# Start addresses of the matmuls' moving operands in a four-layer hybrid trunk

## The chip, the cores and the metric

The kernel runs on one core of a Trainium2 chip. The metric is the device time of one execution, in microseconds (us). Each number given for a kernel as a whole is the median of its runs; the profile is one further execution, with its own time beside it.

## The reference

Four residual layers work on 256 tokens of width 1024 in float32. Layers 0 and 3 mix tokens by an RWKV-7 recurrence, layer 1 by stick-breaking attention, layer 2 by attention over 64 keys picked per query. Each is followed by a SwiGLU feed-forward block (FFN) of inner width 2816.

```python
def swiglu(h, w_gu, w_down):
    g, u = jnp.split(h @ w_gu, 2, axis=-1)
    return (jax.nn.silu(g) * u) @ w_down
...
    for i in range(DEPTH):
        kind, j = i % N_MIXERS, i // N_MIXERS
        h = rms_norm(x, norm_mix[i])
...
        x = x + y
        x = x + swiglu(rms_norm(x, norm_ffn[i]), ffn_w_gu[i], ffn_w_down[i])
```

Most of the arithmetic is matrix products of the 256 tokens with weights that are read from memory once: 401 weight pieces of 512 KB each.

## The kernel before, in words

**Pieces.** `piece` (line 906) brings 128 rows by 1024 columns of weights into a tile of the group `raw`, rounds them to the type fp32r into a tile `wh` (the high part), and puts what the rounding lost into a tile `wl` (the low part). The activations are split in the same way. A product is then built from fp32r matmuls: high by high, high by low, low by high. There are four slots each of `raw`, `wh` and `wl`. A slot of `wh` or `wl` is 1056 columns wide; the piece begins at column 16 of a `wh` slot and at column 4 of a `wl` slot, that is 64 and 16 bytes behind the slot's start, whatever reads it.

**Stationary and moving.** A matmul has a stationary operand, which a weight load puts into the array first, and a moving operand, which is then streamed from SBUF. In the profile's names, `gate<-xg,wh` writes the PSUM tile `gate`, and the two names behind the arrow are its operands, in order of the moving one and the stationary one.

- In `gemm1` and the FFN (lines 948 and 1068) the pieces are stationary and the activations move: `xg` (normed activations, high and low halves side by side), or `h` (the FFN's inner activations, also high and low side by side). One matmul of 512 columns reads high and low together against `wh`, and one of 256 columns reads the high half against `wl`. These two make a pair with the same moving start. The names are `gate`, `up`, `dn` (the down product) and `qk`.
- In `gemm2` and `out_half` the pieces are stationary too, but high and low halves of the activations lie apart, so that three matmuls of 256 columns make a unit: `kp`, `rp`, `po`.
- In `v_gemm` (line 1629) and `by_tokens` (line 1745) it is the other way round: `xg` is stationary and the pieces move, 512 columns at a time: `vps`, `k`, `q`, `qi`.

**The FFN.** For each of 11 blocks of 256 inner columns, `gate` and `up` take 8 pairs per 128 columns, so that a phase has 352 pairs; `h` is spread over three tiles: groups `SA` (blocks 0 to 3), `SZ` (4 to 7) and `PR` (8 to 10). The down product then runs over the 22 halves of `h` for each of 8 output tiles: 172 pairs, and for the last 4 halves of the last tile three matmuls of 256 columns each. Up to two output tiles are worked on in turn.

**Order and addresses.** A planner (`Plan`) records all operations and sets their order on every engine from its own cost table, dependences and a table of nudges. Its costs look at shapes, types and engines, not at addresses. `Plan.emit` then asks a pool for the SBUF tiles, in the order of the names in `LAYOUT` (line 65), and the pool gives each the next free address, in steps of 32 bytes. In the weight products above, each moving read lies a multiple of 1024 bytes behind the start of its tile or piece, so where such a matmul starts to read, modulo 512, is set by where the tile or piece starts.

Of the kernel before, what the change touches and what calls it, by code (L numbers as in the profile page):

```python
# [14 lines left out]
F32R = mybir.dt.float32r  # L15
# [18 lines left out]
PIECE = 1024  # L34
# [22 lines left out]
for _n, _w in CONSTS:  # L57
# [5 lines left out]


LAYOUT = (
    "ones xt0 chmask xt1 xt2 xt3 sqa_0 QC_0 sq_0 s0_0 raw_0 s1_0 t_0 s6_0 raw_1 raw_2 t_1 t_2 t_3 raw_3 wh_0 wl_0 "
    "wh_1 wh_2 wh_3 t2_0 xm_0 t2_1 xm_1 PR_0 xm_2 consts0 wl_1 xm_3 identb t2_2 wl_2 t_4 t2_3 wl_3 s7_0 xb_0 SZ_0 "
    "t2_4 dc_0 vf0 vf1 vf3 vf2 t_5 t_6 t_7 kc0_0 kc1_0 kc2_0 SA_0 eps_rms lim eps_gn vecs omka kks_0").split()


class Region:
# [249 lines left out]
class Plan:  # L321
# [15 lines left out]
    def unit(self, at_once=1, ns=0.0):  # L337

        plan = self

        class Unit:
            def __enter__(self):
                plan.unit_op = Op("tensor")
                plan.unit_op.ns = ns

            def __exit__(self, *_):
                op, plan.unit_op = plan.unit_op, None
                op.cost /= at_once
                op.cost = op.ns or op.cost
                plan._add(op)  # L350

        return Unit()
# [478 lines left out]
def trunk(ctx: ExitStack, tc: tile.TileContext, xT_in, vecs_in, wts, lora_in, consts_in, id32_in, nqk_in, outT, order, layers=None):  # L831
# [11 lines left out]
    def T(shape, group=None, name="t", dtype=F32):  # L843
        return plan.tile(sb, [P] + list(shape), dtype, group, name)
# [7 lines left out]
    def bank(name, group="ps"):  # L852
        return plan.tile(psum, [P, 512], F32, group, name, "psum")
# [8 lines left out]
    ones = T([P], name="ones")  # L862
# [23 lines left out]
    identb = T([P], name="identb", dtype=BF16)  # L886
    eps_rms, eps_gn = T([1], name="eps_rms"), T([1], name="eps_gn")
    anye.memset(eps_rms, 1e-6)
    lim = T([2], name="lim")
# [3 lines left out]
    omka = T([2, NC], name="omka")  # L893
    for j in range(2):
        dve.tensor_scalar(omka[:, j, :], vt[:, VIDX[f"ka{j}"], :], -1.0, 1.0, op0=ALU.mult, op1=ALU.add)
    chmask = T([2 * NCH, C], name="chmask")
# [4 lines left out]
    def f(ap):  # L901
        return ap.bitcast(F32)


    def piece(key):

        i = len(order)
        order.append(key)
        r = T([PIECE], "raw", f"raw{i}")
        sp.dma_start(r, wts[i])  # L910
        h, l = (T([PIECE + 32], g, f"{g}{i}", F32R)[:, at:at + PIECE] for g, at in (("wh", 16), ("wl", 4)))
        anye.copy(h, r)
        dve.tensor_tensor(l, r, f(h), op=ALU.subtract)
        return h, l
# [26 lines left out]
    def v3(t, n):  # L941
        return t.rearrange("p (k m) -> p k m", k=n)
# [12 lines left out]
    def gemm1(key, x, name, group="g"):  # L955


        out = bank(name, group)
        wh, wl = [v3(t, NC) for t in piece(key)]
        for c in range(NC):  # L960
            with unit():
                pe.matmul(out, wh[:, c], flat(x[:, c]), start=(c == 0), stop=False)
                pe.matmul(out[:, :S], wl[:, c], x[:, c, 0], start=False, stop=(c == NC - 1))
        return out

    def gemm2(key, xs, name):

        out = bank(name, "g")
        for c in range(NC):
            if c % 4 == 0:  # L970
                wh, wl = [v3(t, 4) for t in piece(key + (c // 4,))]
            with unit():
                for i in range(2):
                    sl = slice(i * P, (i + 1) * P)
                    mm3(out[:, i * S:(i + 1) * S], (wh[:, c % 4, sl], wl[:, c % 4, sl]), xs(c),
                        start=(c == 0 and i == 0), stop=(c == NC - 1 and i == 1))
        return out

    def out_half(key, half, xs, after):

        for j in range(4):
            o = bank("po", "g")
            wh, wl = [v3(t, 4) for t in piece(key + (half, j))]
            for k in range(4):
                with unit():
                    for n in range(2):
                        sl = slice(n * P, (n + 1) * P)
                        mm3(o[:, n * S:(n + 1) * S], (wh[:, k, sl], wl[:, k, sl]), xs(k),
                            start=(k == 0 and n == 0), stop=(k == 3 and n == 1))
            dve.tensor_tensor(xt[j], xt[j], ab(o), op=ALU.add)  # L990
            if half == 1:
                after(j)
# [636 lines left out]
    def v_gemm(vt_, key, xs, rsc, k):  # L1629

        o = [bank("vps", "g") for tb in range(2)]
        for c in range(NC):
            if c % 2 == 0:
                wh, wl = [v3(t, 2) for t in piece(key + (c // 2,))]
            xh, xl = xs(c)
            with unit():
                for tb in range(2):
                    tsl = slice(tb * P, (tb + 1) * P)
                    pe.matmul(o[tb], xh[:, tsl], wh[:, c % 2, :], start=(c == 0), stop=False)
                    pe.matmul(o[tb], xh[:, tsl], wl[:, c % 2, :], start=False, stop=False)  # L1640
                    pe.matmul(o[tb], xl[:, tsl], wh[:, c % 2, :], start=False, stop=(c == NC - 1))
        for tb in range(2):
            anye.scale(vt_[:, k, tb, :], o[tb], rsc[:, tb:tb + 1])
# [10 lines left out]
    def stick(layer, after):  # L1654
# [13 lines left out]
        for p in range(8):  # L1668
# [9 lines left out]
            for n in {0: [0], 4: [1]}.get(p, ()):  # L1678
                v_gemm(vt_, ("sv", n), xs, rsc, n)
# [32 lines left out]
    def dsa(layer, after):  # L1712
# [21 lines left out]
        for i in range(2):  # L1734
            ct_, st_ = tables(1024 + 256 * i), tables(1152 + 256 * i)
            g = nqk[:, i:i + 1]
# [9 lines left out]
        def by_tokens(n, name):  # L1746

            o = [bank(name, "g") for tb in range(2)]
            for c in range(0, NC, 2):
                wh, wl = [v3(t, 2) for t in piece(("dt", n, c // 2))]  # L1750
                for tb in range(2):
                    tsl = slice(tb * P, (tb + 1) * P)
                    for i in range(2):
                        xh, xl = xs(c + i)
                        with unit():
                            pe.matmul(o[tb], xh[:, tsl], wh[:, i, :], start=(c + i == 0), stop=False)
                            pe.matmul(o[tb], xh[:, tsl], wl[:, i, :], start=False, stop=False)
                            pe.matmul(o[tb], xl[:, tsl], wh[:, i, :], start=False, stop=(c + i == NC - 1))
            return o
# [17 lines left out]
        def queries_keys(kind, half):  # L1777

            o = by_tokens(2 * kind + half, "kq"[1 - kind])
            at = qt_[:, 2 * kind + half]  # L1780
            r = rr[:, 2 * kind + half]
            for tb in range(2):
                anye.scale(at[:, tb], o[tb], rsc[:, tb:tb + 1])
            for tb in range(2):
                sq = t2("sq")
                act.activation(flat(sq), at[:, tb], AF.Square)
                dve.tensor_reduce(r[:, tb], heads(flat(sq)), axis=AX.X, op=ALU.add)
            act.activation(r, r, AF.Ln, bias=eps_rms, scale=1.0 / HD)
            act.activation(r, r, AF.Exp, scale=-0.5)
            if kind == 0:  # L1790
                for i in range(2):
                    anye.scale(rq[:, half, i], r, (1 - 2 * i) * HD ** -0.5)
            for tb in range(2):
                if kind:
                    dve.tensor_tensor(heads(at[:, tb]), heads(at[:, tb]), r[:, tb][:, :, None].to_broadcast([P, 8, HD]), op=ALU.mult)
                turned(at[:, tb], kind, tb, qk_[:, 4 * half:4 * half + 4, kind, tb * P:(tb + 1) * P])


        ips = by_tokens(6, "qi")
        rs, rsc = rstd_bcast(), rstd_col()  # L1800
        wh, wl = [v3(t, 8) for t in piece(("dk",))]
# [57 lines left out]
        for p in range(8):  # L1859
# [4 lines left out]
            if p % 4 == 0:  # L1864
                values = by_tokens(4 + p // 4, "vps")
                for tb in range(2):
                    anye.scale(vt_[:, p // 4, tb], values[tb], rsc[:, tb:tb + 1])
# [10 lines left out]
            for hh in range(2):  # L1878
# [14 lines left out]
                t = bank("pT")  # L1893
# [207 lines left out]
```

## Time and profile before

| what | value |
|---|---|
| median of 3 runs | 1349.35 us (1347.35 to 1350.13) |
| the profiled execution | 1346.9 us, with a span of 1345.0 us |
| granted TensorE clock | 1.000 of full speed over the whole span |
| weight pieces | 401 of 512 KB, 3.9 us median from issue to landing |
| FFN phases | gate and up 182.7 to 303.7 us, dn 303.7 to 365.2 us in layer 0; much the same three times more |

The matmul engine is PE, its weight loads are PEld, the vector engine is DVE, the scalar engine is ACT. A row of the groups names the tiles, the shape of the array used, the columns and the count, then the busy time and the mean duration of one. A matmul's duration runs from its start to a modelled end, so it holds a tail that the next matmul overlaps. The chain of waits, which lists stretches of PE with their length and the number of matmuls, gives the time that each truly takes up.

### The profile page before, as it was taken

To read this page: it belongs to the slowest core of one execution; us is meant where nothing else is said; L and a number is where in the kernel's file an instruction comes from. 1 tells how busy PE (TensorE), PEld (TensorE's weight loads), DVE (VectorE), ACT (ScalarE), POOL (GpSimd) and SP (SyncE) were. 2 spreads that over 40 slices of the span, in tenths; PEclk is the share of its full clock that TensorE was granted. 3 is DMA by queue.
4 is the path that set the end of the run, shared out by engine and by line. 5 is a ranking of instruction groups with operands and counts; after the bars stand their busy time and mean duration, and the time that the engine had idled before them with its cause. 6 is when DMAs were issued, how large, how long until landed. Compare 5 with 4: busy or idle time off the path is not lost.

```text
span 1345.0 us, 26070 instructions
## 1 busy us (share of the span) xinstructions
PE 1324.5 (98%) x10480; PEld 1159.3 (86%) x10480; DVE 1116.6 (83%) x1932; ACT 776.6 (58%) x1301; POOL 9.1 (1%) x22
## 2 busy tenths in 40 slices
PE   9999899999999999999999999999999999999998
PEld 7997798888888898888888788888899877988887
DVE  8998789886676779996679988887589997998864
ACT  7955665555466755444456876555378366655542
POOL 0000000000000000000000000000000000000000
PEclk9999999999999999999999999999999999999999
DMA  6423255665654446565654535666544232556653
GB/s 243 145 81 125 75 174 188 193 198 176 208 171 157 123 152 192 190 192 201 197 185 138 178 129 186 191 193 197 189 128 133 73 112 76 176 188 190 193 189 120
DMA packets 61336, 220.09 MB, mean 164 GB/s; under 512 B 6816, under 2 KB 8352, under 8 KB 60960
## 3 DMA queue, kind: packets, MB, share of 16 engines
q1 hardware_dynamic: 61216, 218.44, 50.6%
q8 instruction: 82, 1.34, 0.4%
q14 instruction: 38, 0.31, 0.1%
HBM read 217.36 MB, written 1.05 MB: 162 GB/s over the span
## 4 chain that ended last, share of the span: by engine, by line
PE 83%; DVE 12%; ACT 3%; issue 1%; DMA 1%; SPq 0%; DVEq 0%; ACTq 0%
PE dn L827 18%; PE gate L827 18%; PE up L827 18%; PE po L827 6%; PE qk L827 3%; PE vps L827 3%; PE kp L827 3%; PE z L827 2%; DVE inv L827 2%; PE q L827 2%; PE k L827 2%; DVE xtmp L827 1%; DVE SB L827 1%; PE rp L827 1%; DVE wl L827 1%
## 5 line engine op out<-in xcount | busy, mean ns | idle before, releaser
L827 ACT CAST wh<-raw 128x1024 fp32r<-128x1024 f32 x351 | 365.9, 1049 | 332.4 <-PE dn L827 93.7
L827 DVE TENSOR_TENSOR wl<-raw,wh 128x1024 fp32r<-128x1024 f32 x383 | 461.1, 1220 | 83.5 <-ACT wh L827 67.1
L827 PE MATMUL gate<-xg,wh 128*128 128x512 f32 x704 | 260.5, 390 | 0.0
L827 PE MATMUL up<-xg,wh 128*128 128x512 f32 x704 | 260.2, 390 | 0.0
L827 PE MATMUL dn<-h,wh 128*128 128x512 f32 (+1 forms) x720 | 244.4, 388 | 0.0
L827 PE MATMUL dn<-h,wl 128*128 128x256 f32 x704 | 196.1, 278 | 0.0
L827 PE MATMUL up<-xg,wl 128*128 128x256 f32 x704 | 194.5, 276 | 0.0
L827 PE MATMUL gate<-xg,wl 128*128 128x256 f32 x704 | 194.5, 276 | 0.0
L827 PEld LDWEIGHTS dn<-h,wh 128*128 128x128 f32 x720 | 134.2, 188 | 29.3
L827 PEld LDWEIGHTS up<-xg,wh 128*128 128x128 f32 x704 | 132.2, 188 | 27.6
L827 PEld LDWEIGHTS gate<-xg,wh 128*128 128x128 f32 x704 | 132.2, 188 | 27.4
L827 PEld LDWEIGHTS dn<-h,wl 128*128 128x128 f32 x704 | 132.3, 188 | 0.0
L827 PEld LDWEIGHTS up<-xg,wl 128*128 128x128 f32 x704 | 132.2, 188 | 0.1
L827 PEld LDWEIGHTS gate<-xg,wl 128*128 128x128 f32 x704 | 132.1, 188 | 0.1
L827 PE MATMUL vp<-xv,raw 128*128 128x256 f32 x256 | 57.4, 382 | 0.6 <-PE qct L827 0.6
L827 ACT CAST h<-gus 128x512 fp32r<-128x512 f32 x42 | 26.1, 621 | 55.3 <-DVE gus L827 55.0
L827 DVE TENSOR_TENSOR gus<-gus,rstd 128x512 f32<-128x512 f32 x88 | 57.0, 683 | 0.1
L827 PEld LDWEIGHTS vp<-xv,raw 128*128 128x128 f32 x256 | 47.8, 190 | 8.1 <-PE qct L827 0.8
L827 DVE TENSOR_TENSOR h<-gus,h 128x512 fp32r<-128x512 f32 x44 | 30.4, 691 | 25.5 <-ACT h L827 25.5
L827 PE MATMUL rp<-prx,wh 128*128 128x256 f32 x256 | 50.3, 296 | 0.0
L827 PE MATMUL kp<-kx,wh 128*128 128x256 f32 x256 | 47.4, 285 | 0.9 <-DVE kx L827 0.8
L827 PE MATMUL po<-yhl,wh 128*128 128x256 f32 x256 | 47.8, 288 | 0.0
(327 smaller groups left out, 2350.6 us busy)
## 6 DMA issues: line engine op xcount, KB each, us to landing
raw<-in_wts_dram SPq DMA_DIRECT2D x401, 512.0 KB, 3.9
lora<-in_lora_dram SPq DMA_DIRECT2D x2, 1280.0 KB, 10.5
xt<-in_xT_dram SPq DMA_DIRECT2D x4, 256.0 KB, 3.7
lora<-in_lora_dram SPq DMA_DIRECT2D x2, 512.0 KB, 6.5
inv<-in_id_dram SPq DMA_DIRECT2D x2, 512.0 KB, 3.5
out_dram<-xt SPq DMA_DIRECT2D x8, 128.0 KB, 1.9
sbt<-in_consts_dram SPq DMA_DIRECT2D x1, 512.0 KB, 3.7
consts<-in_consts_dram SPq DMA_DIRECT2D x1, 288.0 KB, 9.6
```

Of the source, the lines that this page charges most:

```text
L827: getattr(getattr(nc, o.eng), method)(*map(real, args), **{k: real(a) for k, a in kw.items()})
```

## The change

All instructions, their order on every engine and all their waits stay as they are; row by row, the five engines' lists are the same once the numbers in tile names are left out. Two kinds of address change.

```diff
 LAYOUT = (
-    "ones xt0 chmask xt1 xt2 xt3 sqa_0 QC_0 sq_0 s0_0 raw_0 s1_0 t_0 s6_0 raw_1 raw_2 t_1 t_2 t_3 raw_3 wh_0 wl_0 "
-    "wh_1 wh_2 wh_3 t2_0 xm_0 t2_1 xm_1 PR_0 xm_2 consts0 wl_1 xm_3 identb t2_2 wl_2 t_4 t2_3 wl_3 s7_0 xb_0 SZ_0 "
-    "t2_4 dc_0 vf0 vf1 vf3 vf2 t_5 t_6 t_7 kc0_0 kc1_0 kc2_0 SA_0 eps_rms lim eps_gn vecs omka kks_0").split()
+    "identb dc_0 ones xt0 chmask xt1 xt2 xt3 sqa_0 QC_0 sq_0 s0_0 s1_0 raw_0 raw_1 raw_2 raw_3 xb_0 SZ_0 PR_0 SA_0 "
+    "eps_rms lim eps_gn t_0 s6_0 t_1 t_2 t_3 wh_0 wl_0 wh_1 wh_2 wh_3 t2_0 xm_0 t2_1 xm_1 xm_2 consts0 wl_1 xm_3 t2_2 "
+    "wl_2 t_4 t2_3 wl_3 s7_0 t2_4 vf0 vf1 vf3 vf2 t_5 t_6 t_7 kc0_0 kc1_0 kc2_0 vecs omka kks_0").split()
...
-    def piece(key):
+    def piece(key, home=(16, 4)):
...
-        h, l = (T([PIECE + 32], g, f"{g}{i}", F32R)[:, at:at + PIECE] for g, at in (("wh", 16), ("wl", 4)))
+        h, l = (T([PIECE + 32], g, f"{g}{i}", F32R)[:, at:at + PIECE] for g, at in zip(("wh", "wl"), home))
...
-                wh, wl = [v3(t, 2) for t in piece(key + (c // 2,))]
+                wh, wl = [v3(t, 2) for t in piece(key + (c // 2,), (0, 0))]
...
-                wh, wl = [v3(t, 2) for t in piece(("dt", n, c // 2))]
+                wh, wl = [v3(t, 2) for t in piece(("dt", n, c // 2), (0, 0))]
```

With the tiles in the new order, these are the byte addresses in a partition that the built programs give, and what is left of them modulo 512:

| slot | moving operand it holds | before | mod 512 | after | mod 512 |
|---|---|---|---|---|---|
| `xb` | `xg` (gate, up, qk) | 163584 | 256 | 77312 | 0 |
| `SA` | `h` blocks 0 to 3 | 211072 | 128 | 126464 | 0 |
| `SZ` | `h` blocks 4 to 7; `prx` (rp) | 179968 | 256 | 93696 | 0 |
| `PR` | `h` blocks 8 to 10; `kx` (kp) | 116608 | 384 | 110080 | 0 |
| `s0`, `s1` | `yhl`, `ohl` (po), `xv` (vp) | 44160, 56448 | 128 | 44544, 52736 | 0 |
| `xt0` to `xt3`, `sqa`, `sq`, `QC` | float32 operands | 5248 and on | 128 | 5632 and on | 0 |
| `raw` 0 to 3 | none (`vp` loads it as weights) | 52352, 73984, 78080, 85248 | 128, 256, 256, 256 | 60928 and on | 0 |
| `wh` 0 to 3, slot start | pieces in vps, k, q, qi | 89344, 97792, 102016, 106240 | 256, 0, 128, 256 | 155392, 163840, 168064, 172288 | 256, 0, 128, 256 |
| `wl` 0 to 3, slot start | pieces in vps, k, q, qi | 93568, 136320, 143872, 151168 | 384, 128, 0, 128 | 159616, 185984, 193280, 200576 | 384, 128, 256, 384 |

Pieces that are read as moving operand start at the slot's start after the change, and 64 (`wh`) or 16 bytes (`wl`) behind it before. Pieces that are stationary keep their 64 and 16 bytes. The small tiles `t`, `t2` and `xm`, which are moving operands of some float32 matmuls, and `s6` (128 modulo 512 before and after) are not put on multiples of 512.

## The prediction, as it was put on record

> **What bounds the kernel now.** I read the page first: who is busy, and what the chain that ended last is made of.
>
> ```profile
> span 1345.0 us, 26070 instructions
> PE 1324.5 (98%) x10480; PEld 1159.3 (86%) x10480; DVE 1116.6 (83%) x1932; ACT 776.6 (58%) x1301; POOL 9.1 (1%) x22
> ...
> PE 83%; DVE 12%; ACT 3%; issue 1%; DMA 1%; SPq 0%; DVEq 0%; ACTq 0%
> PE dn L827 18%; PE gate L827 18%; PE up L827 18%; PE po L827 6%; PE qk L827 3%; PE vps L827 3%; PE kp L827 3%; PE z L827 2%; DVE inv L827 2%; PE q L827 2%; PE k L827 2%; DVE xtmp L827 1%; DVE SB L827 1%; PE rp L827 1%; DVE wl L827 1%
> ```
>
> PE is busy for 98% of the span and makes up 83% of the chain; gate, up and dn alone are 54%. No instruction moves, so only what each matmul takes can change the time, and a nanosecond on one of these is a nanosecond of the kernel, if the engines that prepare the pieces keep up. The stretches of layer 0 say how much room they have (busy us of PE, PEld, DVE, ACT, POOL; then clock, DMA share, GB/s):
>
> ```profile
> 182.70:303.70 121.00, 121.00 (x714) 107.06 (x713) 108.66 (x169) 63.93 (x84) 0.00 (x0) 1.00 0.59 191
> 303.70:365.20 61.50, 61.50 (x359) 54.00 (x358) 39.66 (x54) 29.86 (x36) 0.00 (x0) 1.00 0.58 190
> ```
>
> In gate and up DVE is busy 108.66 of 121.0 us, so PE could gain some 12 us there (10%) before DVE set the pace; in dn there is far more room.
>
> Next the groups by shape, for the products that the new addresses touch. A matmul's duration has a tail that the next one overlaps, and the tail is the same for equal work, so a difference of means is a difference of pace.
>
> ```profile
> L827 PE MATMUL gate<-xg,wh 128*128 128x512 f32 x704 | 260.5, 390 | 0.0
> L827 PE MATMUL dn<-h,wh 128*128 128x512 f32 x688 | 238.9, 393 | 0.0
> L827 PE MATMUL dn<-h,wl 128*128 128x256 f32 x704 | 196.1, 278 | 0.0
> L827 PE MATMUL gate<-xg,wl 128*128 128x256 f32 x704 | 194.5, 276 | 0.0
> L827 PE MATMUL rp<-prx,wl 128*128 128x256 f32 x128 | 35.9, 281 | 0.0
> L827 PE MATMUL po<-yhl,wl 128*128 128x256 f32 x128 | 35.9, 280 | 0.0
> L827 PE MATMUL kp<-kx,wl 128*128 128x256 f32 x128 | 36.0, 281 | 0.0
> ```
>
> The same work takes longer in dn than in gate: 3 ns more per 512 columns, 2 ns more per 256. Gate reads one tile that starts at 256 modulo 512; dn reads three that start at 128, 256 and 384. The chain of waits, in order of time, gives the true pace (start, us, matmuls):
>
> ```profile
> 281.81 2.38 PE gate L827 x14
> 304.62 60.88 PE dn L827 x354
> 602.11 60.52 PE dn L827 x353
> 921.49 60.56 PE dn L827 x354
> 1280.53 60.60 PE dn L827 x354
> ```
>
> A gate pair takes 2.38 / 7 = 0.340 us.
>
> **Where dn loses it.** Three short windows of one dn phase (groups by shape in the window) tell more than its mean. From the planner's order: at 336.2 to 339.2 us two output tiles take turns and all moving starts are at 128 modulo 512; at 339.30 the first reads from `SZ` (256) come in and alternate with those at 128; at 318.3 to 323.6 the starts are 384 and 128, then 128 alone.
>
> ```profile
> L827 PE MATMUL dn<-h,wh 128*128 128x512 f32 x10 | 3.4, 389 | 0.0
> L827 PE MATMUL dn<-h,wl 128*128 128x256 f32 x10 | 2.8, 276 | 0.0
> ...
> L827 PE MATMUL dn<-h,wh 128*128 128x512 f32 x8 | 2.8, 395 | 0.0
> L827 PE MATMUL dn<-h,wl 128*128 128x256 f32 x7 | 2.0, 280 | 0.0
> ...
> L827 PE MATMUL dn<-h,wh 128*128 128x512 f32 x16 | 5.7, 396 | 0.0
> L827 PE MATMUL dn<-h,wl 128*128 128x256 f32 x16 | 4.5, 279 | 0.0
> ```
>
> In the first window dn has gate's pace, though two outputs take turns, so turns are not what costs. From the moment on when starts differ by 128 modulo 256, a pair costs 6 + 4 = 10 ns more. The third window is a warning: starts that agree modulo 256, and still the slow pace (7 + 3). So the slow pace is something that PE falls into when the residue changes and that can outlast the change. With every `h` tile at 0 the trigger inside dn is gone; whether PE is ever in the slow pace on entering dn is left.
>
> **The change part by part.**
>
> *dn.* A chain stretch of 354 matmuls is 171 pairs and four units of three. At gate's pace that is 171 x 0.340 = 58.1 us, and 4 x 0.355 = 1.4 us for the units (3 x 0.113 by gate's pace for 256 columns, plus 4 to 5 ns each as the wl rows of rp, po and kp show): 59.6. The four phases took 60.88, 60.52, 60.56 and 60.60, so the excess is 1.3 + 1.0 + 1.0 + 1.0 = 4.3 us. That is the most that this term can give if 0 acts like 128, 256 and 384 do; the least is 0, if the slow pace stays as in the third window. Gate, which has only one residue, loses next to nothing, so I take three quarters: -3.3 us.
>
> *Pieces as moving operand.* Rows of the moving side (min/median/max):
>
> ```profile
> L827 PE MATMUL gate<-xg,wh x704: 388/389/587, 182.7 to 1280.0; 128*128 128x512 f32 x176
> L827 PE MATMUL vps<-wh,xg x128: 387/397/581, 372.5 to 764.0; 128*128 128x512 f32 x128
> L827 PE MATMUL vps<-wl,xg x64: 388/393/398, 372.9 to 763.8; 128*128 128x512 f32 x64
> L827 PE MATMUL k<-wh,xg x64: 387/396/400, 676.2 to 730.2; 128*128 128x512 f32 x64
> L827 PE MATMUL q<-wh,xg x64: 387/397/584, 689.7 to 743.4; 128*128 128x512 f32 x64
> L827 PE MATMUL qi<-wh,xg x32: 388/394/482, 662.6 to 675.2; 128*128 128x512 f32 x32
> L827 PE MATMUL k<-wl,xg x32: 388/389/398, 676.4 to 730.0; 128*128 128x512 f32 x32
> ```
>
> `wh` at 64 bytes off takes 5 to 8 ns over gate's median, `wl` 16 bytes off 0 to 4. Brought to 389 all would give 8 x 128 + 7 x 64 + 8 x 64 + 5 x 32 + 4 x 64 = 2400 ns. But the slots themselves are not moved to 512: `wh` then starts at 256, 0, 128, 256 and `wl` at 384, 128, 256, 384, so high and low of a unit often differ by 128 modulo 256, which is what cost dn 6 ns (395 against 389). Between -2.4 us and, should all 288 `wh` reads pay a few ns more, +1 us, I take -0.7 us: most of the two effects cancel.
>
> *gate, up, qk.* One moving tile before and after; 256 becomes 0. If 0 is no better or worse than the three other residues: 0. Bounds are with the rivals.
>
> *kp, rp, po.* Their starts agree already (384, 256, 128 in each), and all have 280 or 281: the residue makes no difference among them. 0.
>
> *The rest.* Engines that write or read the moved tiles:
>
> ```profile
> L827 DVE TENSOR_TENSOR wl<-raw,wh x383: 1199/1218/1258, 13.1 to 1333.4; 128x1024 fp32r<-128x1024 f32 x192
> L827 ACT CAST wh<-raw x351: 1031/1049/1093, 11.0 to 1332.3; 128x1024 fp32r<-128x1024 f32 x176
> L827 PE MATMUL vp<-xv,raw x256: 379/379/483, 85.4 to 1092.4; 128*128 128x256 f32 x128
> ```
>
> These run over `raw` at 128 and 256 and over all slots of `wh` and `wl` with hardly any spread, and a float32 matmul has one duration; 0 for all three, hidden or not. `raw` lands at other addresses; ACT waits for few landings, so a small change there is covered.
>
> The sum: -3.3 - 0.7 = -4.0 us. On the profiled execution, 1346.9 - 4.0 = 1342.9; it lies 2.45 us under the median, so the median goes to 1349.35 - 4.0 = 1345.4 us. Nothing is late next: DVE has its room, and the order is the planner's as before.
>
> **The rivals.**
>
> *A start at 512 is a case of its own* (18%). The fp32r matmul of 256 columns never takes less than 276, while the warm-up's bf16 one of equal shape gets to 272:
>
> ```profile
> L1935 PE MATMUL warm_o<-warm_x x66: 272/283/421, 1.2 to 1132.7; 128*128 128x256 bf16 x66
> ```
>
> So the fp32r stream pays at least 4 ns per 256 columns, at every start that the trace has. No start at 0 is among them. If those 4 ns were the two 512-byte boundaries that 1024 bytes cross from a start off 512, a start on it crosses one fewer, 2 ns less for each of some 6,500 fp32r matmuls: -13 us, with dn's -4 about 1332 us. If all of it went (4 ns per 256 columns, 8 per 512), 2,600 x 8 + 3,800 x 4 = 36 us, and DVE's room in gate and up would still cover it: 1313. Against it: 128, 256 and 384 pay alike, and so do pieces 16 and 64 bytes off (minimum 387 or 388), though they lie across more boundaries of any smaller size.
>
> *Nothing changes* (20%). The slow pace of dn may come from the sequence of products or last by itself, as at 318.3 us; then about 1349 us. [...]
>
> *Gate and up fall into the slow pace* (12%), slower. They keep 0.340 only as long as PE stays in step. If 0 against stationary pieces at 64 and 16 bytes off, which the trace does not have for these slots, were out of step, 1,408 pairs x 10 ns = 14 us: 1363; with half of the pairs 1356. It is slower from 30% of the pairs on, where it eats dn's gain. Against it: 128, 256 and 384 all reach 389 and 276 with the same pieces; for it, the third window shows that the slow pace holds without a change of residue.
>
> **How the numbers follow.** My own case (50%) spans 1344 to 1349, as its terms go from -5.4 to 0; about 1345.4 is the likeliest. About 0.2%, 2.7 us, is what a measurement can tell from no change. My case passes it three times in four, the case of its own always: 0.37 + 0.18 = 0.55 faster. The same: a quarter of mine, all of "nothing", a little of the slow pace: 0.34. Slower: 0.11. For 8 in 10 the range takes my case, nothing, the half-size slow pace, and the 512 case to its 13 us: 1330 to 1355.
>
> **What would show it.** Right: the dn rows come to 389 to 391 and 276, its four chain stretches to 59.6 to 60 us, gate stays at 390 and 276, rp, po and kp at 280 to 281. The 512 case: gate falls under 388 and 275. Slow pace: gate at 395 and 280. "Nothing": dn stays at 393 and 278. The forecast is wrong if gate's rows move at all, or if dn's do not.

## The result, and the profile after

| what | before | after |
|---|---|---|
| median, first comparison | 1349.74 us (1347.35 to 1350.29, 4 runs) | 1342.28 us (1341.22 to 1343.40, 4 runs) |
| ratio, 95% interval | | 0.9950 [0.9934, 0.9966] |
| median, second comparison | 1347.06 us (23 runs) | 1342.65 us (5 runs) |
| ratio, 95% interval | | 0.9964 [0.9951, 0.9977] |
| profiled execution, span | 1346.9 us, 1345.0 us | 1343.4 us, 1341.5 us |

The changed kernel is faster. The two medians differ by 7.5 and by 4.4 us; what both intervals allow is 0.9951 to 0.9966, or 4.6 to 6.6 us. Most of what sets the two differences apart is the kernel before, whose median is 1349.74 us over 4 runs and 1347.06 us over 23. The page first:

```profile
span 1341.5 us, 26070 instructions
PE 1319.9 (98%) x10480; PEld 1157.1 (86%) x10480; DVE 1117.1 (83%) x1932; ACT 776.3 (58%) x1301; POOL 9.3 (1%) x22
...
PE gate L827 18%; PE up L827 18%; PE dn L827 17%; PE po L827 7%; PE vps L827 3%; PE qk L827 3%; PE kp L827 3%; PE z L827 2%; DVE inv L827 2%; PE k L827 2%; PE q L827 2%; DVE xtmp L827 1%; DVE SB L827 1%; PE rp L827 1%; PE chain L827 1%
```

PE lost 4.6 us of busy time, and DVE and ACT nothing (1117.1 for 1116.6 and 776.3 for 776.6); dn went from 18% of the chain to 17%. The groups by shape of the kernel after (busy us, mean ns of one):

```profile
L827 PE MATMUL gate<-xg,wh 128*128 128x512 f32 x704 | 260.3, 390 | 0.0
L827 PE MATMUL dn<-h,wh 128*128 128x512 f32 x688 | 234.4, 389 | 0.0
L827 PE MATMUL dn<-h,wl 128*128 128x256 f32 x704 | 194.4, 276 | 0.0
L827 PE MATMUL gate<-xg,wl 128*128 128x256 f32 x704 | 194.4, 276 | 0.0
L827 PE MATMUL rp<-prx,wl 128*128 128x256 f32 x128 | 35.9, 281 | 0.0
L827 PE MATMUL po<-yhl,wl 128*128 128x256 f32 x128 | 35.9, 280 | 0.0
```

The two rows of dn went from 393 and 278 to 389 and 276, which is gate's pace; the other rows shown here stand where they stood. The chain of waits of the kernel after, in order of time (start, us, matmuls):

```profile
307.21 59.55 PE dn L827 x354
...
920.38 59.59 PE dn L827 x354
...
1278.06 59.56 PE dn L827 x354
```

These three stretches were 60.88, 60.56 and 60.60: 1.33, 0.97 and 1.04 us less. The other phase is cut by a wait in this execution (50.22 us, 295 matmuls, in its longest part); in the profile of the second comparison it is whole:

```profile
600.35 59.56 PE dn L827 x354
```

It was 60.52 us for one matmul fewer, so dn gave 1.33 + 0.96 + 0.97 + 1.04 = 4.3 us. The moving rows of the kernel after (min/median/max):

```profile
L827 PE MATMUL gate<-xg,wh x704: 389/389/584, 185.4 to 1277.6; 128*128 128x512 f32 x176
L827 PE MATMUL vps<-wh,xg x128: 388/392/583, 373.8 to 763.6; 128*128 128x512 f32 x128
L827 PE MATMUL vps<-wl,xg x64: 387/395/398, 374.2 to 763.4; 128*128 128x512 f32 x64
L827 PE MATMUL k<-wh,xg x64: 387/392/404, 676.0 to 729.7; 128*128 128x512 f32 x64
L827 PE MATMUL q<-wh,xg x64: 387/392/581, 689.5 to 742.9; 128*128 128x512 f32 x64
L827 PE MATMUL k<-wl,xg x32: 387/393/398, 676.2 to 729.5; 128*128 128x512 f32 x32
```

High pieces as moving operand came down from 396 or 397 to 392, low ones went up from 389 to 393 (k) and from 393 to 395 (vps). To add up such small pieces I took, for every matmul in the trace, the time from its start to the start of the next, less gate's pace (226.7 ns for 512 columns, 113.3 for 256, that is 340 ns for a pair), and left out matmuls that come out more than 25 ns over it, as waits. What a duration holds beyond that time, its tail, has a median of 161 to 163 ns in every one of these products, before and after. Summed by product, in us:

| | before | after |
|---|---|---|
| dn | 4.66 | 0.23 |
| vps, k, q, qi (pieces move) | 2.11 | 1.53 |
| gate, up, qk | 1.08 | 0.64 |
| kp, rp, po | 6.77 | 6.75 |

That is 5.5 us off the matmuls' pace, but the two profiled executions differ by only 1346.9 - 1343.4 = 3.5 us. Part of the rest is in the first stretch. The windows, before and then after (busy us of PE, PEld, DVE, ACT, POOL; granted clock, DMA share, GB/s):

```profile
10.00:20.00 10.00, 8.84 (x46) 7.57 (x45) 10.00 (x19) 9.10 (x16) 1.34 (x1) 1.00 0.81 333
```

```profile
10.00:20.00 10.00, 7.97 (x31) 6.17 (x29) 9.41 (x21) 8.97 (x16) 1.52 (x1) 0.83 0.85 338
```

In these 10 us the kernel after got 31 matmuls done where the one before did 46; its gate starts at 185.4 us, not at 182.7. The 0.83 is a mean: the granted clock was 0.50 for 3.4 us, and full before and after.

```profile
13.30:16.70 3.40, 3.40 (x8) 2.73 (x9) 3.40 (x7) 3.39 (x4) 0.08 (x1) 0.50 1.04 413
```

The clock is not the whole delay. The first product of the layer, `lora_in`, started at 11.69 us, where it had started at 10.43, so the kernel was 1.3 us late before the clock fell; over the spell at half clock `lora_in` fell back from 1.27 to 2.95 us behind the kernel before, 1.7 us more, and the waits between there and gate made 2.7 us of the 3.0. The profile of the second comparison, of the very same kernel, has 1.00 there, starts gate at 182.6, and has a span of 1340.6 us, 4.4 under before's:

```profile
L827 PE MATMUL gate<-xg,wh x704: 389/389/584, 182.6 to 1276.6; 128*128 128x512 f32 x176
```

So this late start is the execution's and not the change's. Of the 5.5 us that the starts give, 4.4 us show in that span; where the other 1 us goes, among the waits, was not followed.

### The profile page after: what moved, and what is told of

Same layout as the page of the kernel before. It is cut to its first block, busy times and chain, and to the rows that moved or that the text cites. A ratio compares the mean times of both kernels' runs of the same rounds, so it can differ in the third digit from the quotient of the medians.

```text
span 1341.5 us, 26070 instructions
## 1 busy us (share of the span) xinstructions
PE 1319.9 (98%) x10480; PEld 1157.1 (86%) x10480; DVE 1117.1 (83%) x1932; ACT 776.3 (58%) x1301; POOL 9.3 (1%) x22
## 4 chain that ended last, share of the span: by engine, by line
PE 84%; DVE 11%; ACT 2%; issue 1%; DMA 1%; SPq 0%; DVEq 0%; ACTq 0%
PE gate L827 18%; PE up L827 18%; PE dn L827 17%; PE po L827 7%; PE vps L827 3%; PE qk L827 3%; PE kp L827 3%; PE z L827 2%; DVE inv L827 2%; PE k L827 2%; PE q L827 2%; DVE xtmp L827 1%; DVE SB L827 1%; PE rp L827 1%; PE chain L827 1%
## 5 line engine op out<-in xcount | busy, mean ns | idle before, releaser
L827 PE MATMUL dn<-h,wh 128*128 128x512 f32 (+1 forms) x720 | 240.0, 384 | 0.0
L827 PE MATMUL po<-ohl,wh 128*128 128x256 f32 x256 | 47.7, 287 | 0.0
```

The costliest lines, as they stand in the source:

```text
L827: getattr(getattr(nc, o.eng), method)(*map(real, args), **{k: real(a) for k, a in kw.items()})
```

## The experiments

My theory was the prediction's: the moving starts of consecutive matmuls have to agree modulo 256. Its rivals were that a start on 512 is a case of its own, and that the gain comes from the pieces. Twelve kernels were run, in three groups that shared runs of the kernel before (medians 1347.06, 1348.12 and 1347.54 us), and one alone (1348.33). The four with other residues or one tile out of step ran on one chip, the other eight on another, so that each is best read by its ratio to the kernel before beside it.

**The change again**, for the second comparison.

> The changed kernel again, on the chip and beside the runs of the three others. My theory: 5.5 to 7 us under before as its matmuls add up (dn 4.4, pieces about 1, shorter waits 1); a median 7 or more under before would be spread between runs of the start of the program, whose first 40 us differed by 1.9 us between the two traces.

Measured: 1342.65 us, 0.9964 [0.9951, 0.9977], shown above. That is 4.4 us under before, less than the 5.5 to 7 us that I expected.

**The tiles alone.** Moving pieces go back to 64 and 16 bytes off, in both `v_gemm` and `by_tokens`.

```diff
-                wh, wl = [v3(t, 2) for t in piece(key + (c // 2,), (0, 0))]
+                wh, wl = [v3(t, 2) for t in piece(key + (c // 2,))]
```

> The new order of tiles alone; pieces that move keep their 64 and 16 bytes. My theory (dn is slow only while its moving starts differ by 128 modulo 256): dn comes to 389 and 276 and its long chain stretches to 59.6 us, vps, q and k on wh stay at a median of 396 to 397; 4 to 5 us under before, so about 1345. Rival (the pieces carry the gain): dn stays at 393 and 278 with 60.5 to 60.9 us, and the time stays within 2 us of before.

Measured: 1341.65 us, 0.9961 [0.9948, 0.9975], as fast as the whole change. By groups dn is as after, and by the moving rows the pieces are as before:

```profile
L827 PE MATMUL dn<-h,wh 128*128 128x512 f32 x688 | 234.4, 389 | 0.0
```

```profile
L827 PE MATMUL vps<-wh,xg x128: 387/397/584, 371.5 to 761.7; 128*128 128x512 f32 x128
```

**The pieces alone.** The changed kernel with `LAYOUT` of before.

> The old order of tiles; pieces that move begin at column 0. My theory: dn stays at 393 and 278 (60.5 to 60.9 us per stretch), vps, q and k on wh come to 392, on wl they rise to 393 to 395; 0.5 to 1.5 us under before, so about 1348.5. Rival (the pieces carry the gain): 5 us or more under before, about 1343.

Measured: 1346.37 us, 0.9995 [0.9985, 1.0006]. The two halves of the change come apart cleanly: dn stays at before's mean, and the pieces get a little faster (`vps` on `wh` even to 389, where I had expected 392).

```profile
L827 PE MATMUL dn<-h,wh 128*128 128x512 f32 x688 | 238.9, 393 | 0.0
```

```profile
L827 PE MATMUL vps<-wh,xg x128: 388/389/582, 372.6 to 763.4; 128*128 128x512 f32 x128
L827 PE MATMUL vps<-wl,xg x64: 387/395/398, 373.0 to 763.2; 128*128 128x512 f32 x64
```

By starts it is 0.5 us of pace (2.11 to 1.58), less than the runs can tell from nothing.

**Other residues for all.** One tile is moved in `LAYOUT`, so that the whole block of moving tiles lies at 256 modulo 512, or at 384.

```diff
-    "identb dc_0 ones xt0 ... PR_0 SA_0 "
+    "dc_0 ones xt0 ... PR_0 SA_0 identb "
```

```diff
-    "identb dc_0 ones xt0 ... PR_0 SA_0 "
+    "identb ones xt0 ... PR_0 SA_0 dc_0 "
```

> As the changed kernel, but all of the block of moving tiles 256 bytes lower, at 256 modulo 512; tiles behind the block keep their addresses. My theory (agreement counts, not 512): dn at 389 and 276, stretches of 59.6 us, gate and up at 390 and 276, the time as the changed kernel. Rival (multiples of 512 count): dn back at 393 and 278 or gate above 390, 4 us or more over the changed kernel.

> As the changed kernel, but the block of moving tiles 128 bytes lower, all at 384 modulo 512, which is 128 modulo 256. My theory: dn, gate and up as in the changed kernel, 389 to 390 and 276, the same time within 1 us. Rival (multiples of 512, or of 256, count by themselves): dn or gate slower, 4 us or more over the changed kernel.

Measured: 1342.39 us, 0.9960 [0.9947, 0.9973] at 256, and 1343.72 us, 0.9967 [0.9956, 0.9978] at 384. Both have gate at 390 and dn at 389 and 276; at 384:

```profile
L827 PE MATMUL gate<-xg,wh 128*128 128x512 f32 x704 | 260.5, 390 | 0.0
L827 PE MATMUL dn<-h,wh 128*128 128x512 f32 x688 | 234.5, 389 | 0.0
```

A start on a multiple of 512 is nothing special: "a case of its own" is out. By starts, gate, up and qk take 1.33 us at 384 and 0.64 in the changed kernel, the one small difference.

**One tile out of step.** `xb` and `PR` at 384, `SZ` and `SA` at 0; and the control, `xb` and `PR` at 256 against the same 0.

```diff
-    "identb dc_0 ones xt0 ... xb_0 SZ_0 PR_0 SA_0 "
+    "identb ones xt0 ... xb_0 PR_0 dc_0 SZ_0 SA_0 "
```

```diff
-    "identb dc_0 ones xt0 ... xb_0 SZ_0 PR_0 SA_0 "
+    "dc_0 ones xt0 ... xb_0 PR_0 identb SZ_0 SA_0 "
```

> As the changed kernel, but the last blocks of h (and xg and what lies ahead) start at 384 modulo 512 and the other two h tiles at 0: they differ by 128 modulo 256. My theory: the slow pace comes back in dn where PR and the others meet: 391 to 392 and 277, stretches of 60.1 to 60.4 us, 2 to 3 us over the changed kernel. Rival (the order of the products, not the addresses): stretches of 59.6, no loss.

> The same with 256 in place of 128: the last blocks of h and xg at 256 modulo 512, the other two h tiles at 0; they differ modulo 512 and agree modulo 256. My theory: as the changed kernel, 389 and 276, stretches of 59.6 us. Rival (512 is the measure): as its sister with 128, 60.1 us or more.

Measured: 1349.05 us, 1.0005 [0.9997, 1.0014] out of step by 128, and 1344.37 us, 0.9966 [0.9955, 0.9978] out of step by 256. First the kernel with 128, then the one with 256:

```profile
L827 PE MATMUL dn<-h,wh 128*128 128x512 f32 x688 | 239.2, 393 | 0.0
L827 PE MATMUL dn<-h,wl 128*128 128x256 f32 x704 | 196.2, 279 | 0.0
```

```profile
L827 PE MATMUL dn<-h,wh 128*128 128x512 f32 x688 | 234.4, 389 | 0.0
L827 PE MATMUL dn<-h,wl 128*128 128x256 f32 x704 | 194.4, 276 | 0.0
```

Among the starts tried here, all multiples of 128, a difference of 128 costs and a difference of 256 costs nothing: in the second kernel, 172 full-pace pairs were followed by one that starts 256 off, and every one of those kept the pace. The stretches of the first are 60.5 to 61.0 us, more than the 60.1 to 60.4 that I expected, and its pairs show why dn loses more than its changes of start explain. I sorted its dn pairs by the starts of the pair before and the pair behind. Where the start differs from the pair before, at least 86% of the pairs in each class are slow (over 5 ns above 340; 160 pairs). Where all three start alike, where no change is near, still 48% (at 0, 407 pairs) and 67% (at 384, 69 pairs) are. No pair goes from 340 (within 2 ns) to slow without a change of start just before it, neither here nor in the kernel before. A run of slow pairs that no further change prolongs lasts between 1 and 25 pairs and then ends at one stroke, and the next pairs are at 340 again. So the pace is a state that a change of 128 sets off in dn and that outlasts it, which fits that 3 blocks of 11 at another residue cost as much as before's whole mixture.

**Pieces that agree.** The eight slots lie in turn between `PR` and `SA`, `wh` at 0 and 256 modulo 512, `wl` at 128 and 384; low moving pieces begin at column 32, so that all moving starts agree modulo 256. Stationary pieces keep their 64 and 16 bytes.

```diff
-    "... PR_0 SA_0 "
+    "... PR_0 wh_0 wl_0 wh_1 wl_1 wh_2 wl_2 wh_3 wl_3 SA_0 "
...
-                wh, wl = [v3(t, 2) for t in piece(key + (c // 2,), (0, 0))]
+                wh, wl = [v3(t, 2) for t in piece(key + (c // 2,), (0, 32))]
```

> As the changed kernel, but the wh and wl slots lie in turn (each 4224 bytes) and a moving low piece begins at column 32, so that all moving pieces start at a multiple of 256 bytes, half of them off 512. My theory (agreement modulo 256 is what counts): vps, q, k and qi come to a median of 389 on wh and wl alike, 1 to 1.5 us under the changed kernel, about 1341. Rival (a multiple of 512 counts): half of the pieces stay slow, medians of 391 to 395, no gain. Rival (the slow pace there has another cause): no change at 392 and 395.

Measured: 1347.35 us, 1.0003 [0.9995, 1.0012]. The pieces did what the theory says, the median of each is 389, but for `qi` on `wh` (394):

```profile
L827 PE MATMUL vps<-wh,xg x128: 388/389/582, 376.3 to 765.5; 128*128 128x512 f32 x128
L827 PE MATMUL vps<-wl,xg x64: 387/389/396, 376.7 to 765.3; 128*128 128x512 f32 x64
```

By starts they gained 1.0 us on the changed kernel (1.53 to 0.57). But gate, up and qk went from 0.64 to 5.45 and dn from 0.23 to 1.99: with moving starts that agree throughout, products were slow all the same. The prediction's third rival had come up, and instead of the 1341 us that I expected the time was before's. The new places of the slots change the stationary addresses too, so four more kernels take the two sides apart.

**The slots in turn, moving pieces at column 0** (the kernel above with `(0, 0)` in place of `(0, 32)`), and **the low moving pieces at column 32, slots as in the changed kernel** (the changed kernel with `(0, 32)`).

> The run with interleaved slots again (high and low slots in turn, between PR and SA), with the moving pieces at column 0 of both, as in the changed kernel: the two slots of a pair then hold moving pieces that differ by 128 modulo 256. Only the low moving pieces' start differs from that run. Theory (where the stationary slots lie is what slowed gate and up there): gate stays at 394 and 278 to 281, dn at +1.8 ns per 512 columns, and the pieces are slower than there (392 and 395): 1348 to 1350 us, 1.001 of the kernel before. Rival (it was the low moving pieces at column 32): gate is back at 389/276, dn at 59.6 us, pieces 392/395: 1342 to 1343 us, 0.996.

> The changed kernel with one number more: the low moving pieces begin at column 32 (128 bytes) of their slots, the high ones stay at column 0. The slots and everything stationary stay where the changed kernel has them. The low moving pieces then start at 0, 0, 128, 0 modulo 256, like the high ones, where the changed kernel has them at 128, 128, 0, 128. Theory (only the agreement of consecutive moving starts modulo 256 counts): about 10 of 16 neighbouring high and low pieces now agree, so the median of vps<-wl,xg falls from 395 to about 389 to 391, vps<-wh,xg from 392 to 390; gate stays 389/276 and dn 59.5 to 59.6 us; the time is 0.3 to 1 us under the changed kernel's, 0.9955 of the kernel before. Rival (the low moving pieces at column 32 are what put gate and up into the slow pace in the run with interleaved slots): gate reads 394/278 to 281 again, and the time is 1345 to 1349 us, 0.998 to 1.000.

Measured: 1350.22 us, 1.0021 [1.0013, 1.0030] with the slots in turn, and 1343.75 us, 0.9963 [0.9951, 0.9976] with column 32 alone. So column 32 is not the cause: the first FFN is slow without it (slots in turn), and gate is at full pace with it alone. What the two slow kernels share is the new order of `LAYOUT`, which moves the slots and the small tiles behind them. Which of these counts isn't parted here; modulo 512 the stationary starts are even among the changed kernel's own (64 and 320 for `wh`, 144 and 400 for `wl`). Column 32 does its own small work: the low pieces fall from 395 to 389, and gate is untouched.

```profile
L827 PE MATMUL gate<-xg,wh x704: 389/389/584, 186.1 to 1277.9; 128*128 128x512 f32 x176
...
L827 PE MATMUL vps<-wl,xg x64: 387/389/397, 374.9 to 763.6; 128*128 128x512 f32 x64
```

By starts that is 1.53 to 1.17 us; 0.4 us can't be seen in the times. The kernel with the slots in turn is odder. Its chain, four phases of dn, and its moving rows within the windows of the first and of the second FFN:

```profile
308.82 61.26 PE dn L827 x354
...
607.24 59.45 PE dn L827 x353
...
925.62 59.58 PE dn L827 x354
...
1283.75 59.60 PE dn L827 x354
```

```profile
L827 PE MATMUL gate<-xg,wh x176: 394/394/585, 183.5 to 308.3; 128*128 128x512 f32 x176
L827 PE MATMUL gate<-xg,wl x176: 278/281/283, 183.8 to 308.5; 128*128 128x256 f32 x176
...
L827 PE MATMUL up<-xg,wh x176: 389/389/584, 486.4 to 605.7; 128*128 128x512 f32 x176
L827 PE MATMUL up<-xg,wl x176: 276/276/285, 486.7 to 605.9; 128*128 128x256 f32 x176
```

The whole first FFN runs slow, the three others are near full pace: dn 61.26 against 59.45 to 59.60 us. They read the same tiles from the same slots: of dn, the pairs with the first `wh` and the first `wl` slot take 10.05 ns over 340 in the first FFN and 0.00 in the second (44 and 40 pairs). So the addresses of a single matmul do not alone set its pace; something else, which differs between the two FFNs, counts. The starts tell more. Counted until five pairs in a row are within 2 ns of 340, an FFN of the changed kernel begins with 3 to 6 slow pairs of its 524, and one of the kernel before with 1 to 23. In both kernels with the slots in turn the first FFN never gets out, and the three others take 46 to 49 pairs. What these two change is thus how long the pace lasts; what sets it off ahead of an FFN, and what ends it, isn't known.

**Stationary pieces at column 0.** Once with slots of 4096 bytes in turn, so that every operand of these products, moving or stationary, starts on 512; once in the changed kernel's own slots, with one edit.

```diff
-        h, l = (T([PIECE + 32], g, f"{g}{i}", F32R)[:, at:at + PIECE] for g, at in zip(("wh", "wl"), home))
+        h, l = (T([PIECE], g, f"{g}{i}", F32R)[:, at:at + PIECE] for g, at in zip(("wh", "wl"), home))
...
-    def piece(key, home=(16, 4)):
+    def piece(key, home=(0, 0)):
```

```diff
-    def piece(key, home=(16, 4)):
+    def piece(key, home=(0, 0)):
```

> The interleaved slots made 4096 bytes long, and every piece, stationary and moving, at column 0: all moving operands start at 0 modulo 512, and so do all stationary ones of a piece's first block. Theory (moving starts that agree, nothing else): pieces 388 to 390, gate 389/276, dn 59.5 us: 1341 to 1342 us, 0.995 of the kernel before. Rival (stationary starts count as well: with the moving starts all equal it is they that differ or agree with the moving ones): gate in the slow pace, 394/280, as in the run with interleaved slots, or a third value of its own, 1347 us or more. What this run gives for gate beside the other two of this call tells whether it is the stationary pieces' 64 and 16 bytes, or the slots' own places.

> The changed kernel with its stationary pieces at column 0 too (in place of 64 and 16 bytes into their slots); the slots stay where the changed kernel has them, at 256, 0, 128, 256 modulo 512 for the high pieces and 384, 128, 256, 384 for the low ones, and the moving operands do not move. So the stationary operands now start at multiples of 128, and the moving ones at multiples of 512. Theory (the 64 and 16 bytes are what kept the stationary operands out of the moving ones' way): gate and dn read 394 to 395 and 278 to 281 for all pieces, the 256-column matmuls of rp, po and kp lose some 2 ns each, the time is 1360 to 1367 us, 1.010 to 1.015 of the kernel before. Rival 1 (only a stationary operand at the same place modulo 512 as the moving one costs): only the pieces in the slot at 0 are slow, about a quarter of the high ones, 1346 to 1349 us, 0.999 to 1.001. Rival 2 (it was the slots' lying in turn, 4096 bytes apart, and not the columns): gate 389/276, dn 59.6 us, 1342 to 1344 us, 0.996.

Measured: 1366.97 us, 1.0140 [1.0127, 1.0153], and 1363.38 us, 1.0114 [1.0096, 1.0133]. The groups, first with all on 512, then with only the stationary start changed:

```profile
L827 PE MATMUL gate<-xg,wh 128*128 128x512 f32 x704 | 265.8, 396 | 0.0
L827 PE MATMUL dn<-h,wh 128*128 128x512 f32 x688 | 241.3, 395 | 0.0
L827 PE MATMUL gate<-xg,wl 128*128 128x256 f32 x704 | 197.5, 281 | 0.0
...
L827 PE MATMUL po<-yhl,wl 128*128 128x256 f32 x128 | 36.2, 283 | 0.0
```

```profile
L827 PE MATMUL gate<-xg,wh 128*128 128x512 f32 x704 | 264.6, 394 | 0.0
L827 PE MATMUL dn<-h,wh 128*128 128x512 f32 x688 | 240.7, 394 | 0.0
...
L827 PE MATMUL gate<-xg,wl 128*128 128x256 f32 x704 | 197.4, 280 | 0.0
...
L827 PE MATMUL po<-yhl,wl 128*128 128x256 f32 x128 | 36.1, 282 | 0.0
```

gate, up and dn are slow in all four FFNs, by 4 to 6 ns a matmul on average, and po loses 2 to 3 ns. With all on 512 I had expected full pace and 1341 to 1342 us, so the theory that only moving starts count is refuted. The one-edit kernel is 21 us over the changed kernel (1363.38 against 1342.28 and 1342.65). Its slow pairs are not only those in the slot at 0, as rival 1 of that run had it: gate's pairs lose 7 to 10 ns in every slot, those with both pieces at 128 modulo 512 the least. With all on 512 the slow pace has two sizes, about 7 ns a pair in the first and last FFN and 13 in the two between; these are gate's moving rows in the windows of the first and of the second:

```profile
L827 PE MATMUL gate<-xg,wh x176: 391/391/586, 182.7 to 306.6; 128*128 128x512 f32 x176
L827 PE MATMUL gate<-xg,wh x176: 392/398/583, 484.0 to 609.2; 128*128 128x512 f32 x176
```

In the same kernel the pieces that move do well (0.49 us by starts):

```profile
L827 PE MATMUL vps<-wh,xg x128: 388/389/582, 374.9 to 771.5; 128*128 128x512 f32 x128
```

There the stationary operand, a part of `xg`, starts on 512 too. So a stationary start on 512 isn't slow by itself; in these runs it is slow in the products that take turns between 512 and 256 columns, or have only 256. Which of the differences between the products matters, the runs do not show.

The one-edit kernel has the same instructions, moving addresses and order as the changed one, and 64 and 16 bytes of the stationary start are worth some 9 ns a pair (20.0 us on 2,224 pairs). The edit moves the addresses at which ACT and DVE write the pieces as well as those at which PE loads them, so the runs do not show which of the accesses it is, nor whether the memory, the load or the array waits.

## Why the prediction was right or wrong

- **The bound.** PE sets the end, and the others had room: right. A nanosecond a matmul was about a nanosecond of the kernel: the one-edit kernel lost 20.0 us of pace by starts (gate, up and qk 0.64 to 14.29, dn 0.23 to 6.57) and 21 us of time. In the change itself 5.5 us of pace gave 4.4 us of span.
- **dn, -3.3 us (0 to -4.3).** Right in kind, and shown by the tiles alone and by the pair of kernels with one tile out of step; mis-sized by its discount, since it gave all 4.3 us, the end of its range (three quarters of 4.3 would be 3.2, a slip of 0.1). I had taken a quarter off in case PE enters dn in the slow pace. It does not, in the changed kernel: its gate and up leave PE at full pace (gate's median is 389), and nothing in dn disturbs it. That worry fitted the kernel with the slots in turn, where the first dn was slow (61.26 us) behind a gate and up that were slow too (gate at 394).
- **Pieces, -0.7 us (-2.4 to +1).** Right: 0.6 us by starts, and the run with the pieces alone is too near to nothing to confirm it by time. The reason fits as well: `wh` came down from 396 or 397 to 392 without its 64 bytes, and `wl`, up from 389 to 393 (k) and from 393 to 395 (vps), is at 389 or 390 when it starts 128 bytes later, at column 32. The two kernels that make them agree, wholly or in part, get the rest (0.57 and 1.17 us left of 1.53).
- **gate, up, qk, 0.** 0.4 us better by starts, with rows that do not move. **kp, rp, po, 0** and **the rest, 0:** right; DVE's and ACT's busy times stayed within 0.5 us.
- **The sum.** -4.0 us was forecast, from 1349.35 to 1345.4 us; the medians were 1342.28 and 1342.65 us, against 1349.74 and 1347.06 for before. So 4.0 us is a little less than the 4.6 to 6.6 us that both intervals allow. The terms add to 5.5 us by the starts; dn alone is 4.3. Two things are luck. The medians lie under the 1344 us at which I had let my own case end, though the bounds of its two terms add to 6.7 us and not to 5.4; the forecast's range holds them because it goes down to 1330 us, for a start at 512 as a case of its own, which was wrong. And the profiled execution of after came out at 1343.4 where I had 1342.9, but with the late start in it; the second profile, without it, lies at 1342.65.
- **"A start at 512 is a case of its own" (18%).** Wrong: gate's minimum stays at 389 and 276, and 256 and 384 do as well.
- **"Nothing changes" (20%).** Wrong: with the sequence of products as it was, the tiles' addresses alone bring dn to 389 and 276. Half of its reason holds, since the slow pace does last by itself once it is set off, for up to 25 pairs without a further change of start (one tile out of step by 128).
- **"Gate and up fall into the slow pace" (12%).** Not in this change: its FFNs get out of the slow pace within 6 pairs. But the rival is real, and my price held: some 9 to 10 ns a pair, 394 to 396 and 280 to 281 in the rows. A moving start at 0 against pieces at 64 and 16 bytes, where I had placed it, is not enough for it: the changed kernel has both and keeps the pace, and the kernels with the slots in turn have both and lose it in the first FFN. With the stationary pieces at column 0 it is there in all four.

## What to carry to other kernels

Where short matmuls follow one another without a gap, look at the means of equal shapes in different products: a few ns between them, as between 393 in dn and 390 in gate here, can be addresses. Here it paid to let the moving starts of consecutive matmuls agree modulo 256 (a multiple of 512 is more than was needed). When tiles are moved, measure again, since the starts of the stationary operand can count for more: 64 and 16 bytes off a round address were worth 20 us here. Judge it by the start-to-start time of a pair, because a gain of 5 us is as large as the spread of single executions (1345.27 to 1350.52 us for the kernel before in the second comparison).

## What the runs showed of the hardware that was not expected

- The slow pace is a state. The same dn pairs, from the same addresses, took 350 ns in one FFN and 340 in the next (slots in turn), and it can last a whole FFN of 185 us. It has more than one size: 347 and 353 ns a pair in different FFNs of the kernel with all on 512. What ends it isn't known.
- Stationary starts count: 340 ns a pair with the pieces 64 and 16 bytes off, 349 on average with them at column 0, where pairs go from 340 to slow 191 times with no change of the moving start.
- kp, rp and po take 4 to 5 ns a matmul of 256 columns over the 113.3 of gate whatever the moving start, and about 6 in the two kernels with the stationary pieces at column 0. That is 6.8 us of this kernel that none of the runs removed.
- In 8 of the 14 profiled executions the granted clock falls once before the last 2 us of the span. In the changed kernel's first profile it was 0.50 for 3.4 us, and PE fell 1.7 us further behind. Five others have a mean of 0.83 in one window of 10 us, like that one (from 130 us in one of them, from 140 us in four). The two with the pieces that agree and with all on 512 have 0.83 from 1100 to 1120 us, and 0.97 and 0.86 in the two windows of 20 us from 1100 us. By my estimate from these means, at 0.50 that is 3.4 us in each of the five, and 6.8 us in the two.
